# A fourth store behind the last load, and accumulator banks copied out by two engines at once, in a batched matmul

## Chip, cores, metric

One core of one Trainium2 chip. The metric is device time in microseconds (us) of one execution; the profile's span, from the first to the last instruction, is about 2 us shorter. All times in the profile count from the start of the span. TensorE (PE in the views) multiplies; ACT (ScalarE), DVE (VectorE) and Pool (GpSimd) compute and copy; SP issues transfers, as Pool does. "b29" means batch 29 of 0 to 31.

## Reference

```python
batch, m, k, n = 32, 512, 1024, 768          # fp32 inputs and output
np.matmul(x, weight)                         # x [32,512,1024], weight [32,1024,768]
```

One batch reads 2.1 MB of `x` and 3.1 MB of `weight` and writes 1.57 MB. The loads cast to bf16 on the way: 167.77 MB are read, and the loads' part of Pool's queue counts half of that (88.61 MB on q0 in the page below, 4.72 of them held stores).

## The kernel before

Loads go out on Pool's DMA queue four batches ahead. TensorE transposes `x` through the small accumulator `pt`, DVE copies the result to `xT`, and the matmuls of two row blocks (a "pair") fill one accumulator tile `pm` of 1,536 fp32 columns, in three parts of 512 called banks here. `evacuate` copies it to `out_sb`. Most outputs are stored on the SP queue, beside the loads. Those of three late batches are HELD: they go to Pool's queue, which already holds every load, so they move behind the last load (its last mark comes at 501.13, theirs at 504.95, 508.61 and 512.22). The last batch goes out on SP in two halves.

```python
    CHUNKED = {B - 4: (4, 4), B - 3: (4, 4), B - 2: (4, 4), B - 1: (4, 2, 2)}
    HELD = {B - 4, B - 3, B - 2}
    ...
    out_pool = ctx.enter_context(tc.tile_pool(name="out", bufs=5))
    mpsum = ctx.enter_context(tc.tile_pool(name="mpsum", bufs=2, space=bass.MemoryType.PSUM))
    ...
    def evacuate(b, pair, pm):
        o = outs[b]
        nc.scalar.copy(o[:, pair * N2:pair * N2 + 1024], pm[:, 0:1024])
        nc.vector.tensor_copy(o[:, pair * N2 + 1024:(pair + 1) * N2], pm[:, 1024:N2])
    ...
        for b in range(B):
            if b + 4 < B:
                load_x(b + 4)                      # Pool's queue
                load_w(b + 4)
            outs[b] = out_pool.tile([P, MT * N], F32, name="out_sb")
            if b not in CHUNKED:
                ...                                # two pairs: matmuls, evacuate
                nc.sync.dma_start(out_view[b], outs[b])
                continue
            xT = ready.pop(b, None) or {mt: transpose(b, mt) for mt in range(MT)}
            pms = [mpsum.tile([P, N2], F32, name="pm") for _ in range(2)]
            at = 0
            for n in CHUNKED[b]:                   # weights arrive in chunks
                last = at + n == KT
                for mt in range(MT):
                    if last and b + 1 < B:         # x of the next batch
                        ready.setdefault(b + 1, {})[mt] = transpose(b + 1, mt)
                    matmuls(pms[mt // 2], mt % 2, xT[mt], b, range(at, at + n), True)
                    if last and mt % 2 == 1:
                        pair = mt // 2
                        evacuate(b, pair, pms[pair])
                        if b not in HELD:
                            cols = slice(pair * N2, (pair + 1) * N2)
                            nc.sync.dma_start(out_view[b, :, cols], outs[b][:, cols])
                at += n
            if b in HELD:
                nc.gpsimd.dma_start(out=out_view[b], in_=outs[b])
```

## Time and profile before

| | before |
|---|---|
| time, median of the first 3 runs | 520.1 us (519.97 to 521.08) |
| span of the profiled run | 518.8 us (time 520.58) |
| TensorE busy | 425.6 us, 82% |
| moved | 167.77 MB in, 50.33 MB out |

Lines of the page of the kernel before: the mean busy share of the 16 DMA engines in 40 slices (9 is 90% or more), then the DMA queues (packets, MB, share of 16 engines).

```profile
DMA  8999999999999999999999999999999999999996
...
q0 software_dynamic: 10368, 88.61, 79.3%
q1 hardware_dynamic: 4320, 45.61, 21.2%
q8 instruction: 20, 0.33, 0.2%
...
HBM read 167.77 MB, written 50.33 MB: 420 GB/s over the span
```

The DMA engines are the bound: 90% or more busy in every slice but the first and last.

From the table of waits of the kernel before (who waited for whom: us in total, times, longest):

```profile
DVE out_sb L90 <- ACT out_sb L89: 157.7, 36, 8.4
...
PE pm L78 <- DMA w_sb<-in_weight_dram: 58.3, 21, 5.2
...
PE pm L78 <- DVE xT L66: 11.0, 7, 2.1
```

DVE waits for ACT's copy, although it reads and writes other columns. TensorE in turn waits 11.0 us in all for `xT`, which DVE makes after those copies, but five times as long for weights.

The tail is different. Pieces of the chain of waits of the kernel before, 462 to 475 us (start, length, what). A landing that the profile couldn't name is "another core or an unknown queue"; here it is `x` of b29. A transfer leaves 16 completion marks in the trace, read here as one for each DMA engine; the last of this one comes at 468.19.

```profile
462.60 2.76 PE pm L78 x16
465.36 2.83 another core or an unknown queue
468.19 0.14 issue
468.32 1.10 PE pt L64 x4
469.42 2.37 PE pm L78 x8
```

TensorE waits 2.8 us for that load and from then on doesn't wait again. Timeline lines of the kernel before near its end (start, length, engine, line, operation, and in brackets the idle time before it and who ended it):

```profile
503.79 0.53 POOL L137 DMA_DIRECT2D out_dram<-out_sb  x1 [11.77 <-DVE out_sb L90]
...
512.16 1.01 ACT L89 COPY out_sb<-pm 128x1024 f32<-128x1024 f32 x1 [0.29 <-PE pm L78]
512.62 1.63 SPq L134 DMA_DIRECT2D out_dram<-out_sb  x2
513.21 0.69 DVE L90 COPY out_sb<-pm 128x512 f32<-128x512 f32 x1 [0.61 <-ACT out_sb L89]
```

The last held store is issued at 503.79, the two halves of the last batch only at 512.62 and 513.92, after the serial copies. The DMA engines, in the window 509 to 513 of the kernel before (40 slices):

```profile
DMA  9552825229502922005020220000000000000000
```

They run dry and wait for the last copies. That gap is what the change aims at.

### The profile page before, as it was taken

What the parts mean: (1) busy time and instruction counts of PE and PEld (TensorE: products, weight loads), DVE (VectorE), ACT (ScalarE), POOL (GpSimd) and SP (SyncE); (2) the same over time, 40 slices, a digit from 0 to 9 for tenths busy, and PEclk for the clock granted to TensorE, in tenths of its full rate; (3) what the DMA queues carried; (4) which work ended last, traced back from release to release, by engine and by line L of the source; (5) the groups of instructions that cost most, each with busy time, mean ns of one, the idle gap of its engine ahead of it and who ended that gap; (6) DMA issues with size and microseconds to landing.
All of it is one profiled execution on the core that took longest, in us unless ns stands there. A gap on an engine that the chain in (4) does not pass through costs nothing.

```text
span 518.8 us, 5796 instructions
## 1 busy us (share of the span) xinstructions
PE 425.6 (82%) x2512; PEld 278.3 (54%) x2560; DVE 124.2 (24%) x192; ACT 66.1 (13%) x65; POOL 38.9 (7%) x78
## 2 busy tenths in 40 slices
PE   1788789788888878897888978788887879878994
PEld 1455456455555545564555645466554555555662
DVE  1122222222221212212122122122221221223331
ACT  0011111011110101110011101011010110101111
POOL 4000000000000000000000000000000000001000
PEclk9999899798998979998899989799898997998998
DMA  8999999999999999999999999999999999999996
GB/s 159 216 231 268 269 265 277 275 239 272 254 275 278 253 270 241 275 279 273 253 250 262 275 279 247 268 250 275 277 252 273 242 273 278 265 266 229 215 329 250
DMA packets 14713, 134.59 MB, mean 259 GB/s; under 512 B 1632, under 2 KB 1632, under 8 KB 3040
## 3 DMA queue, kind: packets, MB, share of 16 engines
q0 software_dynamic: 10368, 88.61, 79.3%
q1 hardware_dynamic: 4320, 45.61, 21.2%
q8 instruction: 20, 0.33, 0.2%
q14 instruction: 5, 0.04, 0.0%
HBM read 167.77 MB, written 50.33 MB: 420 GB/s over the span
## 4 chain that ended last, share of the span: by engine, by line
PE 80%; another core or an unknown queue 10%; DMA 3%; issue 2%; ACT 2%; DVE 1%; POOL 0%; DVEq 0%; POOLq 0%
PE pm L78 70%; PE pt L64 11%; DMA w_sb<-in_weight_dram 3%; ACT out_sb L89 2%; DVE xT L66 1%; DVE out_sb L90 0%; POOL x_sb L50 0%; DVEq L66 0%; POOLq L152 0%
## 5 line engine op out<-in xcount | busy, mean ns | idle before, releaser
L78 PE MATMUL pm<-w_sb,xT 128*128 128x256 bf16 (+1 forms) x2000 | 372.4, 341 | 72.6 <-DMA w_sb<-in_weight_dram 58.3
L78 PEld LDWEIGHTS <-xT 128*128 128x128 bf16 x2048 | 207.6, 102 | 211.8 <-issue 56.5
L66 DVE COPY xT<-pt 128x1024 bf16<-128x1024 bf16 x128 | 85.2, 686 | 232.0 <-PE pt L64 232.0
L89 ACT COPY out_sb<-pm 128x1024 f32<-128x1024 f32 x64 | 64.8, 1013 | 446.3 <-PE pm L78 446.3
L64 PE MATMUL pt<-ident,x_sb 128*128 128x128 f32 x512 | 80.2, 291 | 13.9 <-DMA x_sb<-in_x_dram 12.5
L64 PEld LDWEIGHTS pt<-ident,x_sb 128*128 128x128 f32 x512 | 76.6, 207 | 21.6 <-issue 15.0
L90 DVE COPY out_sb<-pm 128x512 f32<-128x512 f32 x64 | 44.0, 687 | 157.7 <-ACT out_sb L89 157.7
L56 POOL DMA_DIRECT2D w_sb<-in_weight_dram x37 | 19.7, 531 | 239.2 <-DMA w_sb<-in_weight_dram 204.2
L50 POOL DMA_DIRECT2D x_sb<-in_x_dram x32 | 17.1, 536 | 196.8 <-PE pt L64 133.1
L137 POOL DMA_DIRECT2D out_dram<-out_sb x3 | 1.6, 533 | 29.2 <-DVE out_sb L90 29.2
L89 ACT ACT_TABLE_LOAD x1 | 1.3, 1283 | 0.7 <-PEq L152 0.7
masks.py:199 POOL TENSOR_SCALAR_AFFINE_SELECT ident<-ident 128x128 f32<-128x128 f32 x1 | 0.3, 287 | 0.1
masks.py:197 POOL MEMSET ident<- 128x128 f32 x1 | 0.2, 243 | 0.0
L152 POOL MEMSET const-float32-0.0<- 128x1 f32 x1 | 0.1, 99 | 0.2 <-issue 0.2
L152 POOL MEMSET const-bfloat16-1.0<- 128x1 bf16 x1 | 0.1, 102 | 0.0
L152 POOL MEMSET const-uint8-127<- 128x1 uint8 x1 | 0.1, 102 | 0.0
L152 POOL MEMSET const-float32-1.0<- 128x1 f32 x1 | 0.1, 99 | 0.0
## 6 DMA issues: line engine op xcount, KB each, us to landing
w_sb<-in_weight_dram POOLq DMA_DIRECT2D x28, 1536.0 KB, 63.1
out_dram<-out_sb SPq DMA_DIRECT2D x28, 1536.0 KB, 14.5
x_sb<-in_x_dram POOLq DMA_DIRECT2D x32, 1024.0 KB, 62.1
w_sb<-in_weight_dram POOLq DMA_DIRECT2D x7, 768.0 KB, 48.1
out_dram<-out_sb POOLq DMA_DIRECT2D x3, 1536.0 KB, 17.1
out_dram<-out_sb SPq DMA_DIRECT2D x2, 768.0 KB, 3.5
w_sb<-in_weight_dram POOLq DMA_DIRECT2D x2, 384.0 KB, 29.4
```

Of the source, the lines that this page charges most:

```text
L50: nc.gpsimd.dma_start(out=xs[b], in_=x_view[b])
L56: nc.gpsimd.dma_start(out=ws[b][:, at:at + n, :], in_=w_view[b, :, at:at + n, :])
L64: nc.tensor.transpose(pt[:, j, :], pairs[:, mt, j::JT], ident)
L66: nc.vector.tensor_copy(xT.rearrange("p j m r -> p (j m r)"), pt.bitcast(BF16).rearrange("p j m -> p (j m)"))
L78: nc.tensor.matmul(pm[:, half * N + off:half * N + off + size], xT[:, ko // 2, :, ko % 2], ws[b][:, ko, off:off + size], start=(ko == 0 an ...
L89: nc.scalar.copy(o[:, pair * N2:pair * N2 + 1024], pm[:, 0:1024])
L90: nc.vector.tensor_copy(o[:, pair * N2 + 1024:(pair + 1) * N2], pm[:, 1024:N2])
L137: nc.gpsimd.dma_start(out=out_view[b], in_=outs[b])
L152: nc = _bacc.Bacc("TRN2", target_bir_lowering=False, num_devices=1)
```

## The change

A fourth output (b27) is held back behind the last load, for which a sixth output buffer is needed. The three banks of an accumulator become tiles of their own: ACT copies bank 0, DVE bank 1, ACT bank 2. The intent is to fill the gap at the end, to bring the last loads forward, and to shorten the copies after the last matmul.

```diff
-    HELD = {B - 4, B - 3, B - 2}
+    HELD = {B - 5, B - 4, B - 3, B - 2}
-    out_pool = ctx.enter_context(tc.tile_pool(name="out", bufs=5))
+    out_pool = ctx.enter_context(tc.tile_pool(name="out", bufs=6))
+    def banks():
+        return [mpsum.tile([P, 512], F32, name=f"pm{i}") for i in range(3)]
 ...
-    SPLITS = (((0, 512), (512, N - 512)), ((0, 1024 - N), (1024 - N, N2 - 1024)))
+    SPLITS = (
+        ((0, 0, 0, 512), (1, 0, 512, N - 512)),
+        ((1, N - 512, 0, 1024 - N), (2, 0, 1024 - N, N2 - 1024)),
+    )
 ...                                   # matmuls write pm[bank][:, at:at + size]
     def evacuate(b, pair, pm):
-        o = outs[b]
-        nc.scalar.copy(o[:, pair * N2:pair * N2 + 1024], pm[:, 0:1024])
-        nc.vector.tensor_copy(o[:, pair * N2 + 1024:(pair + 1) * N2], pm[:, 1024:N2])
+        o = outs[b][:, pair * N2:(pair + 1) * N2]
+        nc.scalar.copy(o[:, 0:512], pm[0])
+        nc.vector.tensor_copy(o[:, 512:1024], pm[1])
+        nc.scalar.copy(o[:, 1024:N2], pm[2])
 ...
-                nc.sync.dma_start(out_view[b], outs[b])
+                if b in HELD:
+                    held.append(b)
+                else:
+                    nc.sync.dma_start(out_view[b], outs[b])
                 continue
 ...
             if b in HELD:
-                nc.gpsimd.dma_start(out=out_view[b], in_=outs[b])
+                held.append(b)
+            for h in held:
+                nc.gpsimd.dma_start(out=out_view[h], in_=outs[h])
+            held = []
```

More of the change, by code (lines that the diff above doesn't have):

```diff
@@ L69, in transpose @@
         return xT
-    SPLITS = (((0, 512), (512, N - 512)), ((0, 1024 - N), (1024 - N, N2 - 1024)))
+    SPLITS = (
+        ((0, 0, 0, 512), (1, 0, 512, N - 512)),
+        ((1, N - 512, 0, 1024 - N), (2, 0, 1024 - N, N2 - 1024)),
+    )
     def matmuls(pm, half, xT, b, kos, together):
         for ko in kos:
-            for i, (off, size) in enumerate(SPLITS[half]):
+            for i, (bank, at, off, size) in enumerate(SPLITS[half]):
                 shares = half == 1 and i == 0
                 nc.tensor.matmul(
-                    pm[:, half * N + off:half * N + off + size],
+                    pm[bank][:, at:at + size],
                     xT[:, ko // 2, :, ko % 2],
@@ L99 @@
             load_w(b)
-        ready = {}
+        ready, held = {}, []
         for b in range(B):
@@ L109 @@
                 for pair in range(2):
-                    pm = mpsum.tile([P, N2], F32, name="pm")
+                    pm = banks()
                     for half in range(2):
@@ L117 @@
                     evacuate(b, pair, pm)
-                nc.sync.dma_start(out_view[b], outs[b])
+                if b in HELD:
+                    held.append(b)
+                else:
+                    nc.sync.dma_start(out_view[b], outs[b])
                 continue
             xT = ready.pop(b, None) or {mt: transpose(b, mt) for mt in range(MT)}
-            pms = [mpsum.tile([P, N2], F32, name="pm") for _ in range(2)]
+            pms = [banks() for _ in range(2)]
             at = 0
```

## The prediction

> **What bounds the kernel now.** The DMA engines. The page's slices show them 90% or more busy in all but the first and last of 40; 218 MB move in 518.8 us, 420 GB/s. TensorE is busy 82%; in the table of waits it waits for loads (`w_sb` 58.3 us). The tail differs. In the timeline TensorE last waits at 465.4 us (2.8 us, for the `x` of batch 29, b29 for short, whose last completion mark comes at 468.2), then runs without a break to 512.1. The last load lands at 501.1; the three held stores behind it land at 505.0, 508.6 and 512.2 (slowest of each one's 16 completion marks). Then the engines stand still until the two half stores of the last batch, issued at 512.6 and 513.9, which land at 515.9 and 517.8.
>
> **What the change moves.**
>
> 1. No byte goes. The store of b27 (1.57 MB, 461 to 469 on the SP queue, 47% of the DMA share there, 3.8 us of all 16 engines) moves to the Pool queue behind the last load. Loads after 461 come about 3.7 us earlier; `x` of b29 at about 465.4 (the load before it lands at 460.5, other late `x` loads take 4.9). [...]
>
> 2. Copy-out today is serial: ACT 1.01 us, then DVE 0.69. Now ACT takes bank 0 early, and DVE's bank 1 (0.69) runs beside ACT's bank 2 (about 0.55, an estimate from half of 1.01): 1.0 us less after the last matmul. In steady state DVE gets to the next `xT` 1 us sooner, but loads are the limit there, so it is worth nothing.
>
> 3. TensorE's wait at 465.4 shrinks; it resumes at about 465.5 instead of 468.3 and ends at about 509.3 instead of 512.1. The last two stores are issued at about 508.9 and 510.1.
>
> **How much is critical.** The compute chain gains 3.8 us, the DMA engines don't. Held stores still end at about 512.2 on the slowest engines, because the queues' total work is the same; the fastest are done at 509. The last 1.57 MB takes 3.8 us more: 515.9 on the slow engines, against 517.8. The gain is what the slow engines stand idle today, about 1.9 us; the tail turns from TensorE-bound into DMA-bound to the end. If the lag of 3.3 to 3.9 us between a transfer's first and last completion marks shrank, up to 3.6 us could be won.
>
> **Time.** 520.1 - 1.9 = 518.2 us, range 516.4 to 519.6. Faster by over 2%: 1%; within 2%: 98%; slower by over 2%: 1%.
>
> **What would show it.** Step 1: a last load 3.7 us earlier, four Pool stores in a row, no SP store from 461 to 469. Step 2: DVE's copies no longer wait for ACT (157.7 us in the table of waits today). Step 3: TensorE's end near 509.3. The whole: no idle DMA between the held stores and the last two; the chain of waits ends in DMA, not in copies.
>
> **What would make it wrong.** The copies stay serial because both write one `out_sb` tile: 1 us lost, which the DMA bound hides. Pool stores slower than SP ones, or a fourth queued store that waits for an earlier transfer to land, would eat the gain. If the slow engines lag more, loads don't come earlier and TensorE's wait stands.

Cut from step 1 is a sentence with a rule on how the engines share their time between queues; the traces show the shares alone (54% and 47% in the window 461 to 469 of the kernel before). 517.8 less 515.9 is the gain of 1.9, and 520.1 less 1.9 the forecast of 518.2 us.

## The result

| | before | changed |
|---|---|---|
| median | 520.08 us (519.97 to 521.08, 4 runs) | 519.06 us (518.86 to 519.47, 4 runs) |
| span of the profiled run | 518.8 us | 516.8 us |

The ratio is 0.9977, with a 95% interval of 0.996 to 0.9994: a small gain, inside the predicted range. A ratio is the mean time of one kernel's fast runs over the mean of the other's of the same rounds, so it is not quite the ratio of the medians.

The page of the changed kernel:

```profile
DMA  8999999999999999999999999999999999999997
...
q0 software_dynamic: 10512, 90.18, 80.3%
q1 hardware_dynamic: 4176, 44.04, 20.6%
q8 instruction: 20, 0.33, 0.2%
```

1.57 MB have moved from q1 (SP) to q0 (Pool). The waits of the changed kernel:

```profile
DVE out_sb L97 <- PE pm L85: 115.0, 36, 8.5
...
PE pm L85 <- DMA w_sb<-in_weight_dram: 68.1, 25, 5.2
...
PE pm L85 <- DVE xT L69: 0.9, 3, 0.3
```

DVE now waits for TensorE alone: the copies do run at once. TensorE's waits for `xT` fell from 11.0 to 0.9 us, and its waits for weights grew from 58.3 to 68.1: in the body of the kernel what the copies give back is spent waiting for loads. The chain of waits at the same place:

```profile
463.71 1.69 another core or an unknown queue
465.40 0.14 issue
465.53 0.72 PE pt L67 x4
466.25 1.30 PE pm L85 x8
```

`x` of b29 lands at 465.40 instead of 468.19, and TensorE goes on 2.8 us sooner. The queues in the window 461 to 469, before and then changed, show why: the store on SP is gone from it, and the loads have the engines to themselves.

```profile
q0 software_dynamic: 148, 0.90, 53.9%
q1 hardware_dynamic: 134, 1.57, 47.2%
```

```profile
q0 software_dynamic: 294, 1.70, 102.5%
```

The end of the changed kernel in its timeline:

```profile
498.55 0.53 POOL L150 DMA_DIRECT2D out_dram<-out_sb  x1 [11.77 <-ACT out_sb L98]
...
507.24 2.04 SPq L145 DMA_DIRECT2D out_dram<-out_sb  x2
507.71 0.69 DVE L97 COPY out_sb<-pm 128x512 f32<-128x512 f32 x1 [0.55 <-PE pm L85]
507.93 0.58 ACT L98 COPY out_sb<-pm 128x512 f32<-128x512 f32 x1 [0.17 <-PE pm L85]
```

The last copies overlap (507.71 and 507.93) and end at 508.5 instead of 513.9. Five microseconds of compute chain are gone, but only 2.0 us of span. In the window 509 to 513 the DMA engines of the changed kernel are busy:

```profile
DMA  9897589978799279948978995998786554755455
```

So the end is set by DMA now. The last mark of all is at 515.70; it was 517.76. One sign named in the prediction can't be read: the profile's chain of waits, which was to end in DMA, stops at ACT's last copy (507.93), because it doesn't follow the last store.

One number didn't follow the plan: TensorE saved 4.2 us (from 512.1 to 507.9), not 2.8. Stretches of both kernels after that wait (window, its length; busy us and instructions of PE, PEld, DVE, ACT, POOL; the TensorE clock granted; DMA share; GB/s), before and then changed:

```profile
468.20:470.70 2.50, 2.38 (x9) 1.62 (x10) 0.69 (x1) 0.00 (x0) 0.53 (x1) 0.50 1.02 234
468.20:474.20 6.00, 5.88 (x31) 4.04 (x31) 1.39 (x2) 0.59 (x1) 1.05 (x2) 0.73 1.04 224
```

```profile
465.40:467.90 2.50, 2.37 (x17) 1.87 (x18) 0.69 (x1) 0.37 (x1) 0.53 (x1) 1.00 1.05 216
465.40:471.40 6.00, 5.81 (x39) 4.43 (x41) 2.71 (x4) 1.53 (x3) 1.05 (x2) 1.00 1.05 217
```

After an idle gap of 3.0 us the clock was 0.50, from 2.7 us into the gap (468.05) to 471.46; after the shorter one of 1.8 us it was 1.00, and TensorE ran 39 matrix instructions in 6 us instead of 31. The length of a gap alone doesn't decide: a gap of 3.35 us in the same changed kernel (until 172.98) was followed by 1.00. The half clock cost about 1.4 us here (4.2 less 2.8, an estimate), which the DMA bound hides. The saving of 4.2 us is that of one run: in the profile of the repeat (experiment 5) `x` of b29 lands at 465.58, before TensorE needs it, TensorE doesn't wait there at all, and its last matmul ends at 508.81, 3.3 us earlier than before.

### The profile page after: what moved, and what is told of

It reads as the page before. It is cut to its first block, busy times and chain, and to the rows that moved or that the text cites. A ratio compares the mean times of both kernels' runs of the same rounds, so it can differ in the third digit from the quotient of the medians.

```text
span 516.8 us, 5892 instructions
## 1 busy us (share of the span) xinstructions
PE 424.2 (82%) x2512; PEld 277.6 (54%) x2560; DVE 127.0 (25%) x192; ACT 76.2 (15%) x129; POOL 39.4 (8%) x79
## 4 chain that ended last, share of the span: by engine, by line
PE 76%; another core or an unknown queue 12%; DMA 8%; issue 1%; DVE 1%; POOL 1%; ACT 0%; POOLq 0%
PE pm L85 65%; PE pt L67 11%; DMA w_sb<-in_weight_dram 8%; DVE out_sb L97 0%; DVE xT L69 0%; POOL x_sb L53 0%; POOL w_sb L59 0%; ACT out_sb L98 0%; POOL ident masks.py:199 0%; POOL ident masks.py:197 0%; POOLq L166 0%
## 5 line engine op out<-in xcount | busy, mean ns | idle before, releaser
L85 PE MATMUL pm<-w_sb,xT 128*128 128x256 bf16 (+1 forms) x2000 | 371.9, 341 | 72.0 <-DMA w_sb<-in_weight_dram 68.1
L96 ACT COPY out_sb<-pm 128x512 f32<-128x512 f32 x64 | 37.5, 585 | 290.6 <-PE pm L85 287.2
L98 ACT COPY out_sb<-pm 128x512 f32<-128x512 f32 x64 | 37.5, 586 | 141.0 <-PE pm L85 140.9
```

The source lines that it names most:

```text
L85: nc.tensor.matmul(pm[bank][:, at:at + size], xT[:, ko // 2, :, ko % 2], ws[b][:, ko, off:off + size], start=(ko == 0 and not (together an ...
L96: nc.scalar.copy(o[:, 0:512], pm[0])
L98: nc.scalar.copy(o[:, 1024:N2], pm[2])
```

## Experiments

The theory (A) says: the gain is the time the DMA engines stood idle at the end, filled by the fourth store; the faster copies are hidden behind the queue; what remains is the slowest DMA engines. Rival B: the gain is the 1 us that the copies save after the last matmul. Rival C: the tail is still bound by compute.

"Last mark" is the latest of a transfer's 16 completion marks, "spread" the distance from the first to the last. The times of the variants below are medians; the ratio is always against the kernel before on the same chip in the same rounds.

### 1. The fourth held store alone

```diff
 # the kernel before, with
+    HELD = {B - 5, B - 4, B - 3, B - 2}     # and held[] as in the change
+    out_pool ... bufs=6
```

> The kernel before plus the fourth held store and the sixth output buffer; copies stay serial. Theory A (the gain is the idle time of the slow DMA engines, filled by the held store; the faster copies are hidden behind the queue): the last load lands near 497.2, TensorE ends near 508, the last store is issued near 510 and still finds the slow engines busy until about 512.5; time as the changed kernel's, 519.1 us (within 0.3), span near 516.9. Rival B (the gain is the 1 us that the copies save after the last matmul): time as before, 520.1.

Measured: 518.69 us (518.57 to 518.87), ratio 0.9959 (0.9947 to 0.9971); span 516.8. Its timeline:

```profile
508.51 1.01 ACT L89 COPY out_sb<-pm 128x1024 f32<-128x1024 f32 x1 [0.29 <-PE pm L78]
508.97 2.19 SPq L137 DMA_DIRECT2D out_dram<-out_sb  x2
509.55 0.69 DVE L90 COPY out_sb<-pm 128x512 f32<-128x512 f32 x1 [0.61 <-ACT out_sb L89]
```

The copies are serial and the last store is issued at 510.27, 1.7 us later than in the changed kernel (508.54), yet the last mark is at 515.69 against 515.70. This is the whole gain, without the split banks. Rival B falls.

### 2. The split banks and parallel copies alone

```diff
 # the changed kernel, with
-    HELD = {B - 5, B - 4, B - 3, B - 2}
+    HELD = {B - 4, B - 3, B - 2}
```

> The changed kernel with only three held stores: split banks and copies at once alone. Theory A: x of batch 29 still lands at 468.2, TensorE ends near 512, the last store is issued about 1 us earlier (512.9 instead of 513.9) into an idle queue; span 517.8, time about 519.1, and the two parts don't add up, because together they are capped by the queue. Rival B (the copies are the whole gain): the same time as the changed kernel, and e1 as before. If the copies are worth nothing even here: 520.1.

Measured: 519.67 us (519.3 to 521.07), ratio 0.9983 (0.9969 to 0.9996); `x` of b29 at 467.1, TensorE's end 512.0, last issue 512.67, last mark 516.51. `x` of b29 came 1.1 us earlier than expected, but TensorE waited again for `x` of b30 (2.2 us), so its end is the expected one. As theory A expects, the copies are worth about 1 us only while the queue runs dry at the end; held store and copies don't add up. This kernel has the sixth output buffer too, and its last load lands at 501.40, no earlier than in the kernel before (501.13): the buffer alone does not bring the loads forward.

### 3. A fifth held store

```diff
 # the changed kernel, with
+    HELD = {B - 6, B - 5, B - 4, B - 3, B - 2}
+    out_pool ... bufs=7
```

> The changed kernel with a fifth held store (batch 26) and a seventh output buffer. Theory A: the queue is already full to the end, so loads come another 3.7 us earlier, TensorE ends earlier, and the time stays at 519.1 (within 0.3); the last completion mark stays near 515.7. Rival C (the tail is still bound by compute): about 1 us or more faster again.

Measured: 519.68 us (518.86 to 519.97), ratio 0.9975 (0.9962 to 0.9989); TensorE's end 507.1, last mark 516.12, span 517.5. The last load came 3.6 us earlier (493.51), but TensorE ended only 0.8 us earlier (1.7 us against the repeat), so this run alone says little against rival C. It falls with experiment 1, where the last store is issued 1.7 us later at no cost, and with the first kernel of experiment 9, where TensorE ends 4.7 us earlier for no gain. And theory A expected no loss here, yet the profiled span is 0.7 us over the changed kernel's. Note that the span ends 1.34 us after the last mark here (517.46 and 516.12) and 1.09 after it in the changed kernel. Experiment 10 takes that up.

### 4. Loads and stores on one queue

```diff
 # the changed kernel, with
-                if b in HELD:
-                    held.append(b)
-                else:
-                    nc.sync.dma_start(out_view[b], outs[b])
+                nc.gpsimd.dma_start(out=out_view[b], in_=outs[b])
```

> The changed kernel with every store but the last two halves on the Pool queue, so that loads and stores share one queue. Theory A says that what is left is the lag of 3.5 us between the first and the last completion marks of a transfer. If that lag comes from two queues sharing the engines, it shrinks to under 1.5 us here and the last mark comes up to 1.7 us earlier: time 517.4 to 518.5. If it comes from the engines themselves, the spread stays at 3 us or more and the time at 519.1.

Measured: 518.35 us (518.05 to 519.22), ratio 0.9957 (0.9942 to 0.9972); last mark 515.08. Half of the expectation failed: the spread did not shrink, it was 4.8 to 5.0 us over the last 60 us. Two queues sharing the engines are not what makes the lag. The time is nevertheless among the best: on one queue the store of b27 is issued after the last load by its place in the program, and need not be held.

### 5. The changed kernel again, beside its variants

> The changed kernel itself, unedited, beside its variants on one chip. Theory A: about 1.2 to 1.7 us under the kernel before (ratio 0.997 to 0.9977), last mark near 515.7. Holding alone gave 0.9959 with the same last mark; the split banks add about 0.25 us of the measured time outside the profiled span (2.05 us between time and span, against 1.78 without them), and if that is so it shows again here.

Measured: 519.02 us (518.81 to 519.2, 6 runs), ratio 0.9962 (0.9944 to 0.9979), span 516.8, last mark 515.73; time less span 2.06 to 2.15 us, against 1.73 to 1.84 in the 11 runs of the kernel before. The ratio is better than in the first comparison, mostly because the kernel before varies: 519.7 to 522.5 us in its 44 runs beside these experiments, about 520.1 in most and over 521 in 17 of them. Those slow executions are in the ratios of all these experiments. The changed kernel stayed within 518.8 to 519.5 in all ten runs. Why the kernel before has slow executions is not settled.

### 6. Only two held stores

```diff
+    HELD = {B - 3, B - 2}
```

> The changed kernel with only two held stores (batches 29 and 30); batch 28 goes out in two halves on the SP queue. Theory A: every store that goes back in front of the loads delays the last loads and TensorE by about 3.7 us once the tail is bound by TensorE; with three held it ended at 512.1, with two it ends near 515, the last store is issued near 516 into an idle queue and the time is about 522 to 523.5, 2 us or more slower than the kernel before. If the held stores did nothing for the compute chain, the time would be that of three held, 519.7.

Measured: 523.05 us (522.68 to 524.31), ratio 1.0038 (1.0019 to 1.0058); TensorE's end 517.1, last issue 517.76, last mark 521.60. The time is as expected, TensorE's end 2 us later than expected (the profiled run was the slowest of the six). With fewer held stores the compute chain binds again, and one more store in front of the loads cost 3.4 us against experiment 2 (medians of different rounds).

### 7. Half of the last store on eight engines

```diff
+    if pair == 1:
+        nc.sync.dma_start(to[64:128], frm[64:128])
+        for p in range(0, 64, 8):
+            nc.sync.dma_start(to[p:p + 8], frm[p:p + 8])
```

> The changed kernel with half of the very last store (64 partitions, 393 KB) sent as eight transfers of 8 partitions each[...]. Theory A says that the last mark is set by a slow half of the engines that lags 3.5 us. [...] If engine lag does not set the end, no change, or slower by what nine issues cost.

Cut from it are a rule on which engines a small transfer uses, which no run here shows, and the two forecasts that rested on that rule: a last mark 0.9 us earlier (514.8) or 0.9 us later (516.6), as those engines lag less or more than the others. The 0.9 us was the estimate: 393 KB over 8 engines at 26 GB/s (the 420 of the profile's page over 16 engines) is 1.9 us, less the half that they would have had anyway. What the trace shows is one mark of each small transfer just after its issue and eight later; it can't tell on which engines.

Measured: 520.24 us (520.02 to 520.55), ratio 0.9986 (0.9969 to 1.0004), last mark 517.0. This one missed. The eight small transfers were issued over 5.5 us, the last at 514.92, and the pace of the issues set the end. The 64 partitions sent as one transfer finished at 514.91, 0.8 us earlier than the full store does, but a small one left six of its eight marks between 513.35 and 513.90 and two at 515.40 and 515.60: with a mark read as an engine, slow and fast ones are mixed among those eight. Inconclusive for the question asked.

### 8. Two accumulator tiles instead of three

```diff
+    return [mpsum.tile([P, c], F32, name=f"pm{i}") for i, c in enumerate((1024, 512))]
+    nc.scalar.copy(o[:, 0:1024], pm[0])
+    nc.vector.tensor_copy(o[:, 1024:N2], pm[1])
```

> The changed kernel with the banks in two tiles (banks 0 and 1 in one, bank 2 in another), so that ACT makes one copy of 1024 and DVE one of 512 at once: half of ACT's copies go. The copies run at once if the wait came from the shared accumulator tile; the output tile is still shared. The last copy ends about 1.0 us after the last matmul instead of 0.6. Time as the changed kernel's or up to 0.3 us less: if the time outside the span follows the number of ACT copies, it falls from 2.05 to 1.78 us here; the last mark stays near 515.7.

Measured: 519.05 us (518.83 to 519.34), ratio 0.9963 (0.9945 to 0.998), last mark 515.92; time less span 1.99 to 2.24 us. DVE's line in its table of waits:

```profile
DVE out_sb L97 <- PE pm L85: 122.3, 36, 8.5
```

DVE waits for TensorE, not for ACT, though both still write one output tile. So the shared accumulator tile made the old wait, and two tiles are enough to end it. Halving ACT's copies did not bring the 0.3 us outside the span back, so the number of copies isn't their cause.

### 9. Fewer and more instructions for TensorE

Who is slow among the DMA engines? The lag grows through the whole kernel: the spread of a transfer is 0.7 us for the first load and 3.5 us for the last. The largest other traffic is the instructions themselves: the 20 packets of 16 KB on q8. In the changed kernel the times of these packets repeat with a period of eight to within 0.02 us (0.89, 0.89, 0.93, 0.93, 0.92, 0.96, 0.96, 0.95 us, and again). The reading tested here takes this as packets dealt to eight engines in turn; twenty then give four engines three and four engines two. The marks of the very last store of the changed kernel, less the first one:

```
0.00 0.10 0.16 0.18 0.19 0.27 0.29 1.37 | 2.18 2.37 2.40 2.45 | 2.90 3.25 3.29 3.45
```

With a mark read as an engine: seven without lag, one with about 1.4, four with about 2.3, four with about 3.2.

The loads of the changed kernel show the lag growing packet by packet (marks less the load's first). Before the first packet (32.6 us) none is over 0.73 us late. After the eighth (208.6) eight marks are 0.97 to 1.58 late; after the sixteenth (407.6) eight are 2.07 to 2.67 late; after the nineteenth (478.0) three marks are at 3.16 to 3.51 and five at 2.34 to 2.68. The repeat of the kernel shows the same counts after the sixteenth and the nineteenth. A packet holds 16,384 bytes, and 1,536 more instructions bring six more packets, 256 each, in the second kernel below (the changed kernel's page has 5,072 instructions on TensorE beside its 20 packets, 254 each). Whether the packets cost time is what this pair of kernels tests. The first kernel leaves out the transposes of all batches but one.

```diff
 # fewer (wrong on purpose)              # more (correct)
 def transpose(b, mt):                    for _ in range(392 if b == 0 else 52 if b < 23 else 0):
+    if b > 0: return first[mt]         +     nc.tensor.ldweights(spare)   # one column
```

> Wrong on purpose: the changed kernel without the transposes of batches 1 to 31 (they reuse the transposed x of batch 0), so that TensorE's stream is about 1,000 instructions shorter; every load and store stays. Reading of the traces so far: the slow DMA engines are those that also carry the 20 instruction packets of 16 KB (queue q8, 0.93 us each[...]), in turn over 8 engines, so 4 of them carry three and 4 carry two, and each packet leaves its engine about 1.1 us behind for good. With 16 packets every one of the 8 carries two: the spread of the last transfers falls from about 3.5 us to about 2.4 us and the last mark from 515.7 to about 514.6; time about 1 us under the changed kernel, near 518.0. If the lag has another cause: spread and last mark as in the changed kernel (515.7), time 519.0.

> Correct: the changed kernel with 1,536 useless weight loads of one column on TensorE in batches 0 to 22, placed where it waits for data; about 26 instruction packets instead of 20. By the same reading two of the 8 engines carry four packets now: the last mark goes from 515.7 to about 516.8 and the time up by about 1.1 us, near 520.1, although TensorE ends its last matmul before 511. If the lag has another cause: last mark near 515.7, time 519.0. Void if TensorE ends after 512, because then its extra work binds.

The queue's line in the pages of the kernel with fewer and of the kernel with more instructions:

```profile
q8 instruction: 16, 0.26, 0.2%
```

```profile
q8 instruction: 26, 0.43, 0.3%
```

With 16 packets the last store's marks, less the first one, are

```
0.00 0.03 0.07 0.20 0.33 0.41 0.55 0.69 | 2.13 2.35 2.37 2.42 2.48 2.54 2.61 2.63
```

The two slow groups have become one, as the deal of two for each predicts, and the last mark is at 514.69 (expected 514.6). So these marks fit the reading that the slow engines are those that carry the instructions. Three cautions. This kernel also has less work on TensorE and DVE, and its result is wrong (relative error 1.39); its bytes of data are the same. The packets are not the whole lag: with the same 20 of them the one-queue kernels of experiments 4 and 11 have a spread of 4.9 and 5.0 us at the last load, against 3.5 to 4.0 in the others, and why is open. And with 26 packets the last mark came at 516.14, not 516.8, no later than in a kernel with 20 (516.12 in experiment 3): the eight slow engines lag 3.1 to 3.6 us there, all alike, and no pair stands out with four. That trace does not confirm the reading; the first of the 26 packets falls at 8.2 us, before the load stream has landed anything (8.7), and may have cost nothing, which is argued and not shown.

The times say something else. More: 520.13 us (519.27 to 520.47), ratio 0.9987 (0.997 to 1.0004), 1.1 us over the changed kernel's 519.02 of other rounds, as expected. Its profiled run was the fastest of its six; TensorE ended at 508.2 in it, so its extra work did not bind there. That the packets, and not the added instructions in some other way, made the 1.1 us is not shown. Fewer: 519.47 us (519.38 to 519.81), ratio 0.9978 (0.996 to 0.9996), no faster than the changed kernel although its last mark is 1 us earlier. The lag is shortened and the time is not: something else ends the kernel.

### 10. The last two stores on Pool's queue

SP's last waits, in the kernel with fewer fetches and then in the changed kernel; the line of code named in them is that of the closing barrier, after which, in the changed kernel, PE, ACT, DVE and SP go on together at 516.18 to 516.19:

```profile
SPq L181 <- PEq L181: 2.2, 2, 1.8
```

```profile
SPq L177 <- PEq L177: 0.7, 2, 0.5
```

In the first one SP is done at 515.01 and waits for another engine. The trace has it: Pool's closing drain, an instruction whose record starts with Pool's last issue (498.53 and 498.55 in the changed kernel), runs until 516.58. In the changed kernel it ends at 515.76, just before SP is done (516.02). So there are two ends, and this experiment moves one of them.

```diff
-    nc.sync.dma_start(out_view[b, :, cols], outs[b][:, cols])
+    nc.gpsimd.dma_start(out=out_view[b, :, cols], in_=outs[b][:, cols])
```

> The changed kernel with its last two half stores issued on the Pool queue too, behind the four held ones. The traces so far show a second end beside the last completion mark: Pool's closing drain instruction ends 2.9 to 3.1 us after the last mark of the Pool queue wherever stores of both queues are mixed (515.76 against 512.73 in the changed kernel; 516.58 against 513.55 in the kernel with fewer fetches, where it and not the last mark set the end). If that is a cost of the Pool queue itself, the last mark stays near 515.7 here, the drain ends near 518.7, the span is near 519.4 and the time near 521.5: about 2.5 us slower than the changed kernel, 1 us slower than the kernel before. If the drain only happens to end there, span and time stay as the changed kernel's, 516.8 and 519.0.

Measured: 521.8 us (521.69 to 522.17), ratio 1.0019 (0.9998 to 1.004); last mark 516.23, drain until 519.34, span 520.1. SP's wait for the barrier in this kernel:

```profile
SPq L177 <- PEq L177: 3.4, 2, 2.9
```

The same bytes through the same engines end 3.3 us later in the profiled span, and 2.8 us in median time against the 519.02 of other rounds, when they close on Pool's queue. The two ends of the kernels, read from the traces of the profiled runs (us; "SP done" is when SP's own waits for its stores are over):

| kernel | TensorE ends | last SP issue | last mark, Pool's queue | Pool's drain ends | SP done | span |
|---|---|---|---|---|---|---|
| before | 512.12 | 513.92 | 512.22 | 515.21 | 518.02 | 518.79 |
| changed | 507.89 | 508.54 | 512.73 | 515.76 | 516.02 | 516.79 |
| 1 fourth store alone | 508.47 | 510.27 | 511.99 | 515.02 | 516.01 | 516.77 |
| 2 copies alone | 512.02 | 512.67 | 512.42 | 515.41 | 516.77 | 517.53 |
| 3 five held | 507.14 | 507.79 | 513.62 | 516.68 | 516.50 | 517.46 |
| 4 one queue | 508.56 | 509.20 | 511.39 | 515.52 | 515.22 | 516.27 |
| 9 fewer fetches | 503.22 | 503.87 | 513.55 | 516.58 | 515.01 | 517.37 |
| 10 last on Pool | 507.92 | none | 516.23 | 519.34 | 516.59 | 520.13 |

The span ends 0.75 to 0.79 us after the later of the two ends in every row. The drain follows the last mark of Pool's queue by 3.0 to 3.1 us, and by 4.1 in experiment 4, where nearly all stores are on that queue. Rows 3 and 9 are now explained as far as the end goes: there the drain binds, not the last mark. (It binds in row 4 too, and in experiment 11, where it ends at 515.62 and SP is done at 515.29: the fastest kernels end on Pool's drain.) What rows 3 and 9 have in common is an early TensorE, so that the SP stores run while held stores are still under way (last SP issue 507.79 and 503.87, last mark of Pool's queue 513.62 and 513.55); that this is why Pool's queue ends later in them is argued, not shown.

### 11. The parts that paid, together

```diff
 # the kernel of experiment 1 (one accumulator tile, serial copies), with
-                if b in HELD:
-                    held.append(b)
-                else:
-                    nc.sync.dma_start(out_view[b], outs[b])
+                nc.gpsimd.dma_start(out=out_view[b], in_=outs[b])
```

> The best of the parts: four stores behind the last load by way of one Pool queue for loads and stores, the old single accumulator tile and serial copies. Theory A: the copies are hidden, so this is the all-Pool kernel (span 516.3, time 518.35) less the 0.3 us that the split tiles add outside the span: span about 516.3, time about 518.1, ratio near 0.995, 2.0 to 2.5 us faster than the kernel before. If serial copies matter here, about 1 us slower than the all-Pool kernel, 519.3.

Measured: 518.02 us (517.95 to 518.37, 6 runs), ratio 0.995 (0.9933 to 0.9966), span 516.4, last mark 515.15. This is the fastest kernel, 2 us under the kernel before and about 1 us under the changed one, though not timed in the same rounds as the latter (519.02 and 519.06). It is also the simplest: all stores but the last two on Pool's queue, old copies.

## Why the prediction was right

**The bound.** "The compute chain gains 3.8 us, the DMA engines don't." Shown: experiment 1 issues its last store 1.7 us later than the changed kernel and ends at the same mark. Predicted last mark 515.9, measured 515.70 and 515.73; predicted landing of `x` of b29 465.4, measured 465.40.

**Step 1, the moved store.** Right in each item: the last load landed at 497.15 instead of 501.13 (4.0 us earlier, predicted 3.7), with no SP store from 461 to 469.

**Step 2, the copies.** The time from the last matmul to the end of the copies fell from 1.8 to 0.6 us, near the 1.0 predicted; ACT's 512 columns took 0.585 us, estimated 0.55. That they are worth nothing beside the held store is experiment 1, and that they are worth about 1 us without it is experiment 2. The feared dependence through `out_sb` isn't there (experiment 8).

**Step 3, TensorE's end.** Predicted 509.3, measured 507.9 (508.8 in the repeat). The mis-sized term is the stretch after the wait: 31 matrix instructions in 6 us at a granted clock that began at 0.50, against 39 at 1.00. The prediction carried the old pace over.

**The size.** Predicted gain 1.9 us; 1.0 us between the medians at first, and a ratio that means 2.0 us (0.38% of 520) in the repeat. In the profiled runs it was 2.0 us of span. That this is so near 1.9 is in part luck: the 27 executions of the kernel before under 521 us, of the 44 beside the experiments, have a median of 520.1 us and a span of 518.4, so that the changed kernel (519.0, span 516.9) gains 1.1 us of time and 1.5 of span on them; the 2.0 of the repeat owes the rest to the slow executions of the kernel before. The difference in the first comparison adds up from three parts: the profiled execution of the kernel before (520.58) was 0.5 us above that kernel's median; that of the changed kernel (518.86) 0.2 us below its own; and the time outside the span rose by 0.3 us, from 1.78 to about 2.1. That last part appears in the kernels with split tiles (medians of 1.9 to 2.1 us) and in none with the old tile (1.77 and 1.76 in experiments 1 and 11). Its cause stays open.

**What the prediction didn't know.** "If the lag ... shrank, up to 3.6 us could be won" is not borne out. With 16 instruction packets instead of 20 the last mark came 1 us earlier (514.69 against 515.70) and the time not at all (519.47 against 519.02): Pool's drain ended 3.0 us after its own queue's last mark there (516.58 and 513.55), later than SP (515.01).

## What to carry to other kernels

When transfers bind and stores can wait, queue enough of them behind the last load to keep the engines fed through the last computation (the fourth held store alone: ratio 0.9959); after that, a faster compute tail was worth nothing here, and a change that bundles both parts should be timed part by part. At a kernel's end look for every engine's last act: here the last bytes belonged on SP's queue, because Pool's closing drain ended 3.0 to 3.1 us after its own queue's last mark (4.1 with nearly all stores on it), and moving the last two stores there cost 2.8 us of time (521.8 against 519.02, in other rounds). The marks of the changed kernel's last store lie 3.45 us apart, and 20 packets of the program's own instructions (16 KB, 0.93 us each) went through the engines beside the data.
